# Opening of a hybrid layer: modulation weights of channel blocks 2 to 7 loaded and multiplied for two blocks at a time

## The chip, the cores and the metric

The kernel runs on one core of one Trainium2 chip. The metric is the device time of one execution in microseconds (us), as the median of several runs. A core has five engines that work at the same time and wait for each other through semaphores: TensorE (PE: matmuls into the PSUM memory; PEld in a profile is its loading of the stationary operand), VectorE (DVE), ScalarE (ACT), GpSimd (POOL) and SyncE (SP, which here only issues transfers). Each takes its instructions in the order in which they stand in its queue.

## The reference

One transformer layer on 512 tokens of 1024 channels, in float32: a gated FFN, a mixer of two attention-like branches, and a second gated FFN, each with its own norm and its own shift, scale and gate, that come from a condition vector c. The opening of the kernel computes the first lines of it:

```
mod = jax.nn.silu(c) @ w_ada + b_ada
sh1, sc1, g1, sh2, sc2, g2, sh3, sc3, g3 = [m[:, None, :] for m in jnp.split(mod, N_MOD, axis=-1)]
u = rms_norm(x, ffn1_norm_g) * (1 + sc1) + sh1
x = x + 0.5 * g1 * swiglu(u, ffn1_w_in, ffn1_w_out)
```

`w_ada` is 1024 x 9216. For the first norm the kernel needs only its first 2048 columns, those of sh1 and sc1: 8.4 MB.

## The kernel before

The 1024 channels are eight blocks k = 0 to 7 of 128, the 512 tokens four blocks of 128. The opening (`start`) runs through the channel blocks: it makes the normed, scaled and shifted input u of block k with channels on the partitions, and multiplies it by the rows k of the first three column blocks of both halves of `ffn1_w_in`, summing over k in six PSUM banks. All data are float32, and a matmul of float32 accuracy is made of three in a faster format, from high and low parts: `uh` and `ul` of u, `wh` and `wl` of the weights.

For one block k the steps are these, with the lines of the kernel before:

- SP loads `ar` (L710), the 1024 x 128 columns of `w_ada` for the shift and the same for the scale, as 128 partitions x 8 rows x 2 x 128 numbers, so in pieces of 512 bytes; and `raw` (L715), two pieces of 128 x 384 of the FFN weights.
- The product c times `ar` is a sum over 1024 rows. Its eight parts of 128 rows are multiplied by a number per partition and added up on DVE (L791 the first, L789 the others, one call for shift and scale together, 128 x 256), in a chain in which each call reads what the last one wrote; for some blocks ACT does the first part (L787). The sum over the 128 partitions is a matmul of the result by a column of ones, one each for shift and scale (`total`, L798). In blocks 1 and 2 some of the eight parts are summed by such matmuls on PE straight from `ar` (L780) and DVE has the others.
- ACT turns the two columns into shift and gain (`mods`, L802 and L803, 128 x 1 each).
- PE transposes the normed x of block k into a PSUM bank (`turn`, L748). ACT reads it twice, with the gain and the shift: into `uh` (L808, rounded) and `uf` (L809, full). DVE subtracts them: `ul` (L811).
- ACT rounds the FFN weights into `wh` (L815), DVE subtracts: `wl` (L819).
- PE does 18 matmuls of 128 x 512 (`mms`, L829): six with `uh` and `wh`, six with `uh` and `wl`, six with `ul` and `wh`.

The order of each engine's queue is written out by hand: each call is tied to follow the one before it on its engine (`queued`), so the text of `start` is the order. In the steady part (k from 3) PE's queue has the first six matmuls of block k-1, the transposes of block k, six more matmuls, `total(k)`, and the last six matmuls of block k-1, which run while ACT makes shift, gain and `uh` of block k. There is one free PSUM bank for the transposes. The four totals' columns of an even and an odd block lie side by side in one other bank (`cb`).

After the opening `cols_rest` transposes a few constants (L188), and the column blocks of the FFN follow, with matmuls at L115 to L117.

Of the kernel before, what the change touches and what calls it, by code (L numbers as in the profile page):

```python
# [20 lines left out]
P = 128  # L21
# [3 lines left out]
NK = 8  # L25
# [23 lines left out]
class Layer:  # L49
# [639 lines left out]
    def start(self, st, tp):  # L689
# [14 lines left out]
        ars, raws, accs, wsp, ms, bt = {}, {}, {}, {}, {}, {}  # L704
        def ada_load(k):
            r = ars[k] = st.tile([P, NK, 2, P], F32, name=self.nm("ar"), tag="ar", bufs=8)
            step = NK if k else 4
            for v in range(2):
                for i0 in range(0, NK, step):
                    spq(lambda: nc.sync.dma_start(r[:, i0:i0 + step, v, :], w_ada[i0 * P:(i0 + step) * P, v * D + k * P:v * D + (k + 1) * P]  # L710
                                                  .rearrange("(i p) n -> p i n", p=P)))
# [8 lines left out]
        ada_load(2)  # L720
# [56 lines left out]
        wide = lambda ap: ap.to_broadcast([P, P])  # L777
        def ada_pe(k, ks, v, first, last):
            for i in ks:
                pe(lambda: PE.matmul(cb[:, col(k, v):col(k, v) + P], ars[k][:, i, v, :], wide(self.ccol[:, i:i + 1]),  # L780
                                     start=first and i == ks[0], stop=last and i == ks[-1]))
        def product(k, i, eng):
            if not i:
                accs[k] = st.tile([P, 2, P], F32, name=self.nm("ac"), tag="ac", bufs=3)
            r, cc = ars[k][:, i], self.ccol[:, i:i + 1]
            if eng is AC:
                act(lambda: AC.activation(accs[k], r, AF.Copy, scale=cc))  # L787
            elif i:
                dve(lambda: V.scalar_tensor_tensor(accs[k], r, cc, accs[k], op0=MUL, op1=ADD))  # L789
            else:  # L790
                dve(lambda: V.tensor_scalar(accs[k], r, cc, None, op0=MUL))  # L791
# [3 lines left out]
        def total(k, more=()):  # L795
            for v in range(2):
                ada_pe(k, more, v, True, False)
                pe(lambda: PE.matmul(cb[:, col(k, v):col(k, v) + P], accs[k][:, v, :], wide(self.one), start=not more, stop=True))  # L798
# [6 lines left out]
        def uh(k):  # L805
            m = ms[k]
            uf[k] = self.tmp(tp, "uf")
            act(lambda: AC.activation(self.uh[k], bt[k], AF.Identity, scale=m[:, 1:2], bias=m[:, 0:1]))  # L808
            act(lambda: AC.activation(uf[k], bt[k], AF.Identity, scale=m[:, 1:2], bias=m[:, 0:1]))  # L809
# [52 lines left out]
        wl(1)  # L862
        wh(2)
        ada_dve(2, range(0, 2))
        ul(1)
        ada_dve(2, range(2, 6))
# [3 lines left out]
        mms(1, 6, 12)  # L870
        total(2, range(6, 8))
        wl(2)
        mods(2)
        uh(2)
        wh(3)
        ada_dve(3, range(0, 3))
        ul(2)
        wl(3)
        ada_dve(3, range(3, 8))
        mms(1, 12, 18)  # L880
        for k in range(3, NK):
            more, early = k < NK - 1, k > 3
# [3 lines left out]
            total(k)  # L886
            if more:
                product(k + 1, 0, AC)
                if early:
                    wh(k + 1)  # L890
                    wl(k + 1)
                ada_dve(k + 1, range(1, 4))
            mods(k)
            uh(k)
            ul(k)
            if more:
                if not early:
                    wh(k + 1)
                    wl(k + 1)
                ada_dve(k + 1, range(4, 8))  # L900
# [602 lines left out]
```

## Time and profile before

| | us |
|---|---|
| median of 3 runs | 1333.47 |
| lowest and highest | 1333.05, 1334.53 |
| the profiled execution | 1333.42 |
| its span, first to last instruction | 1331.6 |
| first matmul at L829 (block 0) | 16.87 |
| first matmul at L829 of block 2 | 30.26 |
| of block 4 | 43.73 |
| of block 6 | 54.66 |
| L188, behind the last matmul of the opening | 65.30 |

In a timeline each row has the start in us from the span's start, the length in us, the engine, the line, the operation, the tile it writes and those it reads, the shapes and how many instructions were put together; in brackets how long the engine stood idle before, and what ended that. A line "A <- B" of the waits says that A waited for B. Rows of groups have the count, the summed busy time, the mean length in ns, and the idle time before. PE's matmuls overlap: each shows about 0.39 us, while they start 0.23 us apart.

### The profile page before, as it was taken

The numbers are of one execution on the slowest core, as the hardware profiler recorded it, in microseconds if no ns is written. First come the engines' busy times: TensorE is split into PE (matmuls) and PEld (weight loads), VectorE is DVE, ScalarE is ACT, GpSimd is POOL, SyncE is SP. The second block draws the span as 40 slices with busy tenths as digits, with TensorE's granted clock in tenths as the row PEclk, the third lists the DMA queues.
The fourth block names the chain that finished last, engine by engine and source line by source line (L and its number), as shares of the span: only waits on it lengthen the run. The fifth ranks groups of instructions, "written<-read, shape, count | busy, mean of one in ns | idle before, by whom it ended". The sixth has DMA issues, their size and how long they took to land.

```text
span 1331.6 us, 17899 instructions
## 1 busy us (share of the span) xinstructions
PE 1312.8 (99%) x6468; PEld 1102.8 (83%) x6468; DVE 945.8 (71%) x1775; ACT 631.3 (47%) x1080; POOL 85.9 (6%) x140
## 2 busy tenths in 40 slices
PE   7999999999999999999999999999999999999998
PEld 6688888888888888988888878888888888888887
DVE  6777677688678867887685976777676565655655
ACT  5533433336557735566575686432354333433442
POOL 2000000001020000000000000002120000000000
PEclk9999999999999999999999999999999999999999
DMA  9776576777662434443343442787537555444474
GB/s 297 226 269 220 168 236 205 255 234 239 215 161 81 135 111 124 134 116 123 80 143 88 112 124 77 227 256 236 160 101 267 185 175 163 145 151 150 153 253 147
DMA packets 228621, 231.11 MB, mean 174 GB/s; under 512 B 12274, under 2 KB 183954, under 8 KB 228532
## 3 DMA queue, kind: packets, MB, share of 16 engines
q1 hardware_dynamic: 217428, 186.34, 46.4%
q0 software_dynamic: 11040, 43.61, 8.8%
q8 instruction: 51, 0.84, 0.2%
q14 instruction: 38, 0.31, 0.1%
q10 hardware_dynamic: 64, 0.02, 0.0%
HBM read 199.97 MB, written 29.95 MB: 173 GB/s over the span
## 4 chain that ended last, share of the span: by engine, by line
PE 91%; DVE 3%; ACT 2%; DMA 2%; issue 1%; SPq 0%; POOL 0%; ACTq 0%; DVEq 0%; POOLq 0%
PE g L117 21%; PE g L116 21%; PE g L115 21%; PE t L472 2%; PE t L474 2%; PE t L473 2%; PE t L1232 2%; PE t L446 1%; PE t L447 1%; PE t L445 1%; PE t L1202 1%; PE t L115 1%; PE t L117 1%; PE t L116 1%; PE g L829 1%
## 5 line engine op out<-in xcount | busy, mean ns | idle before, releaser
L96 ACT ACTIVATE wh<-raw 128x1024 fp32r<-128x1024 f32 x218 | 226.5, 1043 | 387.6 <-PE g L116 97.4
L116 PE MATMUL g<-ul,wh 128*128 128x512 f32 (+2 forms) x984 | 369.9, 376 | 1.1 <-DVE ul L255 0.8
L115 PE MATMUL g<-uh,wh 128*128 128x512 f32 (+2 forms) x984 | 370.1, 377 | 0.1
L117 PE MATMUL g<-uh,wl 128*128 128x512 f32 (+2 forms) x984 | 369.4, 376 | 0.2 <-DVE wl L98 0.2
L98 DVE TENSOR_TENSOR wl<-raw,wh 128x1024 fp32r<-128x1024 f32 x218 | 263.4, 1211 | 141.5 <-ACT wh L96 130.1
L116 PEld LDWEIGHTS g<-ul,wh 128*128 128x128 f32 (+1 forms) x984 | 185.0, 188 | 34.7 <-DVE ul L255 1.0
L117 PEld LDWEIGHTS g<-uh,wl 128*128 128x128 f32 (+1 forms) x984 | 184.9, 188 | 34.0 <-DVE wl L98 0.4
L115 PEld LDWEIGHTS g<-uh,wh 128*128 128x128 f32 (+1 forms) x984 | 184.7, 188 | 34.2 <-ACT sl L368 0.5
L115 PE MATMUL g<-wh,uh 128*128 128x512 f32 (+1 forms) x320 | 111.9, 350 | 0.0
L116 PE MATMUL g<-wl,uh 128*128 128x512 f32 (+1 forms) x320 | 111.0, 347 | 0.0
L117 PE MATMUL g<-wh,ul 128*128 128x512 f32 (+1 forms) x320 | 111.0, 347 | 0.0
L296 DVE SCALAR_TENSOR_TENSOR acc<-raw,ccol,acc 128x1024 f32<-128x1024 f32 (+1 forms) x63 | 66.0, 1065 | 43.0 <-DMA raw<-in_w_ada_dram 42.7
L117 PEld LDWEIGHTS g<-wh,ul 128*128 128x128 f32 x320 | 60.5, 189 | 7.8
L115 PEld LDWEIGHTS g<-wh,uh 128*128 128x128 f32 x320 | 60.5, 189 | 7.7 <-DVE tk L1085 0.5
L116 PEld LDWEIGHTS g<-wl,uh 128*128 128x128 f32 x320 | 60.5, 189 | 7.3
L369 DVE TENSOR_TENSOR hp<-g,sl 128x512 f32<-128x512 f32 x43 | 29.5, 689 | 51.6 <-PE g L117 50.8
L116 PE MATMUL g<-yl,wh 128*128 128x512 f32 x128 | 49.8, 389 | 0.0
L115 PE MATMUL g<-yl,wh 128*128 128x512 f32 x128 | 49.8, 389 | 0.0
L117 PE MATMUL g<-yl,wl 128*128 128x512 f32 x128 | 49.8, 389 | 0.0
L422 ACT ACTIVATE wh<-rw 128x1024 fp32r<-128x1024 f32 x22 | 23.3, 1058 | 49.0 <-issue 31.5
L1184 ACT ACTIVATE S<-S,mn 128x128 f32<-128x128 f32 (+1 forms) x64 | 35.5, 556 | 16.0 <-DVE mn L1176 8.9
L1446 POOL TENSOR_TENSOR sg<-sg,ta 128x512 f32<-128x512 f32 x8 | 13.6, 1694 | 452.4 <-DMA raw<-in_w_branch_b_dram 421.2
(339 smaller groups left out, 2252.1 us busy)
## 6 DMA issues: line engine op xcount, KB each, us to landing
raw<-in_ffn_w_in_dram SPq DMA_DIRECT2D x82, 512.0 KB, 4.7
raw<-in_w_ada_dram SPq DMA_DIRECT2D x56, 512.0 KB, 4.3
raw<-in_w_mix_dram SPq DMA_DIRECT2D x48, 512.0 KB, 3.9
rw<-in_ffn_w_out_dram POOLq DMA_DIRECT2D x20, 1024.0 KB, 6.8
S_d<-rw POOLq DMA_DIRECT2D x22, 768.0 KB, 4.0
raw<-S_d SPq DMA_DIRECT2D x30, 512.0 KB, 3.6
raw<-in_w_mix_dram SPq DMA_DIRECT2D x32, 256.0 KB, 3.9
ar<-in_w_ada_dram SPq DMA_DIRECT2D x14, 512.0 KB, 7.6
```

The source lines that it names most:

```text
L96: self.last_hi = nc.scalar.activation(hi, src, AF.Copy)
L98: self.last_lo = self.last_wl = (eng or nc.vector).tensor_tensor(lo, src, hi, op=SUB)
L115: mm(ps, lh, rh, start=start, stop=False)
L116: mm(ps, lh, rl, start=False, stop=False)
L117: self.last_mm = mm(ps, ll, rh, start=False, stop=stop)
L296: nc.vector.scalar_tensor_tensor(a, r[:, cut(i)], self.ccol[:, k:k + 1], a, op0=MUL, op1=ADD)
L369: nc.vector.tensor_tensor(h, ps_b[:, c0:c1], s[:, :c1 - c0], op=MUL)
L472: mm(ps[t], a[0], wh[:, k, :], start=first and c + k == 0, stop=False, skip_group_check=True)
L473: mm(ps[t], a[0], wl[:, k, :], start=False, stop=False, skip_group_check=True)
L474: mm(ps[t], a[1], wh[:, k, :], start=False, stop=end, skip_group_check=True)
L1184: nc.scalar.activation(S[:, ws], S[:, ws], AF.Exp, scale=-1.0, bias=m, accum_out=sm[:, qb:qb + 1])
L1232: nc.tensor.matmul(po[:, q0:], vt[pr][:, kb, i % 2, :], Px[:, o:o + T - q0], start=n == 1, stop=n == 8)
```

## The change

Blocks 2 and 3, 4 and 5, and 6 and 7 become pairs. The `ar` of a pair is one tile of 128 x 8 x 2 x 256, loaded by two transfers of 1 MB (one each for shift and scale), whose pieces are 1024 bytes long, in place of four transfers of 512 KB. It stands on SP's queue ahead of the FFN weights of both blocks. A product covers both blocks, 128 x 512 in place of 128 x 256, so there are eight per pair, not sixteen; ACT still does the first of pairs 4/5 and 6/7. The totals of both blocks follow each other on PE, and so do both `mods` on ACT. In the first pair DVE does six of the eight products (before, six for block 2 and all eight for block 3) and PE two for both blocks. The order of all four queues is rewritten to fit.

The core of the diff:

```diff
-        def ada_load(k):
-            r = ars[k] = st.tile([P, NK, 2, P], F32, name=self.nm("ar"), tag="ar", bufs=8)
+        def ada_load(*ks):
+            k, n = ks[0], len(ks) * P
+            r = st.tile([P, NK, 2, n], F32, name=self.nm("ar"), tag=f"ar{n}", bufs=2 if n == P else 3)
+            for i, kk in enumerate(ks):
+                ars[kk], accs[kk] = r[:, :, :, i * P:(i + 1) * P], (ks, i)
+            wide[k] = r
...
         def product(k, i, eng):
-            if not i:
-                accs[k] = st.tile([P, 2, P], F32, name=self.nm("ac"), tag="ac", bufs=3)
-            r, cc = ars[k][:, i], self.ccol[:, i:i + 1]
+            n = wide[k].shape[3]
+            if k not in acs:
+                acs[k] = st.tile([P, 2, n], F32, name=self.nm("ac"), tag=f"ac{n}", bufs=1 if n == P else 2)
+            r, cc = wide[k][:, i], self.ccol[:, i:i + 1]
...
-        def uh(k):
+        def uh(k, mid=lambda: None):
             m = ms[k]
             uf[k] = self.tmp(tp, "uf")
             act(lambda: AC.activation(self.uh[k], bt[k], AF.Identity, scale=m[:, 1:2], bias=m[:, 0:1]))
+            mid()
             act(lambda: AC.activation(uf[k], bt[k], AF.Identity, scale=m[:, 1:2], bias=m[:, 0:1]))
...
-        for k in range(3, NK):
-            ada_load(k)
-            if k < 6:
-                load(k)
-        load(6)
-        load(7)
+        load(3)
+        for k in (4, 6):
+            ada_load(k, k + 1)
+            load(k)
+            load(k + 1)
...
         wl(1)
+        ul(1)
+        ada_dve(2, range(0, 6))
         wh(2)
-        ada_dve(2, range(0, 2))
-        ul(1)
-        ada_dve(2, range(2, 6))
+        wh(3)
 
         mms(1, 0, 6)
         turn(2, range(NT))
-        mms(1, 6, 12)
-        total(2, range(6, 8))
+        mms(1, 6, 18)
+        total(2, (6, 7))
+        total(3, (6, 7))
+        mods(2)
+        mods(3)
         wl(2)
-        mods(2)
+        wl(3)
         uh(2)
-        wh(3)
-        ada_dve(3, range(0, 3))
         ul(2)
-        wl(3)
-        ada_dve(3, range(3, 8))
-        mms(1, 12, 18)
         for k in range(3, NK):
-            more, early = k < NK - 1, k > 3
             mms(k - 1, 0, 6)
             turn(k, range(NT))
             mms(k - 1, 6, 12)
-            total(k)
-            if more:
-                product(k + 1, 0, AC)
-                if early:
-                    wh(k + 1)
-                    wl(k + 1)
-                ada_dve(k + 1, range(1, 4))
-            mods(k)
-            uh(k)
-            ul(k)
-            if more:
-                if not early:
-                    wh(k + 1)
-                    wl(k + 1)
-                ada_dve(k + 1, range(4, 8))
+            if k % 2 == 0:
+                total(k)
+                total(k + 1)
+                mods(k)
+                mods(k + 1)
+            uh(k, lambda: product(k + 1, 0, AC) if k % 2 and k < NK - 1 else None)
+            if k % 2 and k < NK - 1:
+                wh(k + 1)
+                wh(k + 2)
+                ada_dve(k + 1, range(1, 3))
+                ul(k)
+                ada_dve(k + 1, range(3, 8))
+                wl(k + 1)
+                wl(k + 2)
+            else:
+                ul(k)
             mms(k - 1, 12, 18)
```

What the change moves shows best in the instruction lists of each engine's queue. The names carry running numbers. PE around the first totals of block 2, before: `uh_155`, `ul_163` and `wh_382` belong to block 1, `uh_156` to block 2, and `t_176` is the bank of the totals.

```order
L829 MATMUL t_175<-uh_155,wl_383 128x512
L780 MATMUL t_176<-ccol,ar_191 128x128 x2
L798 MATMUL t_176<-one,ac_416 128x128
L780 MATMUL t_176<-ccol,ar_191 128x128 x2
L798 MATMUL t_176<-one,ac_416 128x128
L829 MATMUL g_170<-ul_163,wh_382 128x512
L829 MATMUL g_171<-ul_163,wh_382 128x512
L829 MATMUL g_172<-ul_163,wh_382 128x512
L829 MATMUL g_173<-ul_163,wh_382 128x512
L829 MATMUL t_174<-ul_163,wh_382 128x512
L829 MATMUL t_175<-ul_163,wh_382 128x512
L829 MATMUL g_170<-uh_156,wh_413 128x512
```

And now:

```order
L835 MATMUL t_175<-ul_163,wh_373 128x512
L784 MATMUL t_176<-ccol,ar_191 128x128 x2
L803 MATMUL t_176<-one,ac_405 128x128
L784 MATMUL t_176<-ccol,ar_191 128x128 x2
L803 MATMUL t_176<-one,ac_405 128x128
L784 MATMUL t_176<-ccol,ar_191 128x128 x2
L803 MATMUL t_176<-one,ac_405 128x128
L784 MATMUL t_176<-ccol,ar_191 128x128 x2
L803 MATMUL t_176<-one,ac_405 128x128
L835 MATMUL g_170<-uh_156,wh_412 128x512
```

The last six matmuls of block 1 moved ahead of the totals, and the totals of block 3 stand behind those of block 2, right before the matmuls of block 2.

DVE from `ul` of block 3 to the products of block 5, before (`ac_493` is block 4's sum, `ac_538` block 5's):

```order
L811 TENSOR_TENSOR ul_165<-uf_501,uh_157 128x512
L819 TENSOR_TENSOR wl_506<-raw_344,wh_505 128x768
L789 SCALAR_TENSOR_TENSOR ac_493<-ar_341,ccol,ac_493 128x256 x4
L819 TENSOR_TENSOR wl_541<-raw_350,wh_540 128x768
L789 SCALAR_TENSOR_TENSOR ac_538<-ar_347,ccol,ac_538 128x256 x3
L811 TENSOR_TENSOR ul_166<-uf_550,uh_158 128x512
L789 SCALAR_TENSOR_TENSOR ac_538<-ar_347,ccol,ac_538 128x256 x4
```

And now, from `ul` of block 2, with `ac_484` the sum of the pair 4/5:

```order
L817 TENSOR_TENSOR ul_164<-uf_461,uh_156 128x512
L794 SCALAR_TENSOR_TENSOR ac_484<-ar_338,ccol,ac_484 128x512 x2
L817 TENSOR_TENSOR ul_165<-uf_482,uh_157 128x512
L794 SCALAR_TENSOR_TENSOR ac_484<-ar_338,ccol,ac_484 128x512 x5
L825 TENSOR_TENSOR wl_488<-raw_341,wh_487 128x768
L825 TENSOR_TENSOR wl_491<-raw_344,wh_490 128x768
L817 TENSOR_TENSOR ul_166<-uf_536,uh_158 128x512
```

All seven products of a pair on DVE now stand between `ul` of one even block and `wl` of the next, with `ul` of the odd block among them.

ACT now, from the pair 2/3 to the pair 4/5:

```order
L807 ACTIVATE m_453<-t_176,colC 128x1
L808 ACTIVATE m_453<-t_176,colC 128x1
L807 ACTIVATE m_456<-t_176,colC 128x1
L808 ACTIVATE m_456<-t_176,colC 128x1
L813 ACTIVATE uh_156<-t_424,m_453 128x512
L815 ACTIVATE uf_461<-t_424,m_453 128x512
L813 ACTIVATE uh_157<-t_471,m_456 128x512
L792 ACTIVATE ac_484<-ar_338,ccol 128x512
L815 ACTIVATE uf_482<-t_471,m_456 128x512
L821 ACTIVATE wh_487<-raw_341 128x768
L821 ACTIVATE wh_490<-raw_344 128x768
L807 ACTIVATE m_530<-t_176,colC 128x1
```

Four small steps now stand ahead of the first `uh` of a pair, and the first product of the next pair (`ac_484`) stands between `uh` and `uf` of the odd block.

More of the change, by code (lines that the diff above doesn't have):

```diff
@@ L703, in start @@
         sh = [P, 2, NJ0 * P]
-        ars, raws, accs, wsp, ms, bt = {}, {}, {}, {}, {}, {}
-        def ada_load(k):
-            r = ars[k] = st.tile([P, NK, 2, P], F32, name=self.nm("ar"), tag="ar", bufs=8)
+        ars, raws, accs, wsp, ms, bt, wide, acs = {}, {}, {}, {}, {}, {}, {}, {}
+        def ada_load(*ks):
[4 more added lines that the diff above has]
+            wide[k] = r
             step = NK if k else 4
@@ L709, in ada_load @@
                 for i0 in range(0, NK, step):
-                    spq(lambda: nc.sync.dma_start(r[:, i0:i0 + step, v, :], w_ada[i0 * P:(i0 + step) * P, v * D + k * P:v * D + (k + 1) * P]
+                    spq(lambda: nc.sync.dma_start(r[:, i0:i0 + step, v, :], w_ada[i0 * P:(i0 + step) * P, v * D + k * P:v * D + k * P + n]
                                                   .rearrange("(i p) n -> p i n", p=P)))
@@ L719, in start @@
         load(1)
-        ada_load(2)
+        ada_load(2, 3)
         load(2)
@@ L797, in total @@
                 ada_pe(k, more, v, True, False)
-                pe(lambda: PE.matmul(cb[:, col(k, v):col(k, v) + P], accs[k][:, v, :], wide(self.one), start=not more, stop=True))
+                pe(lambda: PE.matmul(cb[:, col(k, v):col(k, v) + P], acs[accs[k][0][0]][:, v, accs[k][1] * P:(accs[k][1] + 1) * P], bcast(self.one), start=not more, stop=True))
         def mods(k):
```

10 lines of the change are left out of this document (5 added, 5 removed).

## The prediction

> **What bounds the kernel now.** First the span, then who waits in the opening (16 to 65 us of the span, where the change lies), then one round of it in order of time.
>
> ```profile
> span 1331.6 us, 17899 instructions
> ```
>
> ```profile
> ACT m L802 <- PE t L798: 18.1, 7, 3.5
> DVE ul L811 <- ACT uf L809: 8.5, 8, 2.8
> PEld g L829 <- ACT uh L808: 4.5, 8, 1.4
> PEld t L798 <- DVE ac L789: 4.0, 5, 1.8
> ...
> DVE ac L791 <- DMA ar<-in_w_ada_dram: 1.8, 2, 1.6
> ...
> ACT ac L787 <- DMA ar<-in_w_ada_dram: 0.8, 1, 0.8
> ```
>
> The columns are total us, times, longest. The large entries are engines waiting for engines. The modulation weights (ar) delay someone by only 2.6 us. So transfers do not pace the opening; a ring of engines does. One turn of it, block 5 to block 6, from the timeline (start, length):
>
> ```profile
> 47.08 0.71 PE L798 MATMUL t<-one,ac 128*128 128x128 f32 x4
> ...
> 49.84 0.69 DVE L811 TENSOR_TENSOR ul<-uf,uh 128x512 fp32r<-128x512 f32 x1 [0.51 <-ACT uf L809]
> 50.45 2.04 DVE L789 SCALAR_TENSOR_TENSOR ac<-ar,ccol,ac 128x256 f32<-128x256 f32 x4
> 52.55 0.52 PEld L798 LDWEIGHTS t<-one,ac 128*128 128x128 f32 x4 [0.29 <-DVE ac L789]
> ```
>
> A turn lasts 52.55 - 47.08 = 5.47 us: total on PE, m and uh on ACT, ul and four products on DVE, next total. PE has nearly as much work, so its weight load waits only 0.29. Behind the opening PE is full, as this window shows (length of the window, then busy time of PE, PEld, DVE, ACT and POOL, granted clock, share of the DMA engines, GB/s), so whatever the opening loses or gains passes to the end.
>
> ```profile
> 90.00:100.00 10.00, 10.00 (x46) 8.29 (x45) 5.21 (x6) 2.61 (x3) 0.00 (x0) 1.00 0.68 250
> ```
>
> **The first pair: weights, products, totals.** The change first differs at block 2. Rows of the timeline of before:
>
> ```profile
> 19.45 0.85 ACT L815 ACTIVATE wh<-raw 128x768 fp32r<-128x768 f32 x1 [0.74 <-DMA raw<-in_ffn_w_in_dram]
> 22.85 0.35 DVE L791 TENSOR_SCALAR ac<-ar,ccol 128x256 f32<-128x256 f32 x1 [1.56 <-DMA ar<-in_w_ada_dram]
> 24.66 0.69 DVE L811 TENSOR_TENSOR ul<-uf,uh 128x512 fp32r<-128x512 f32 x1 [0.94 <-ACT uf L809]
> 27.13 0.64 PEld L780 LDWEIGHTS t<-ccol,ar 128*128 128x128 f32 x4
> 28.58 0.76 PEld L829 LDWEIGHTS g<-ul,wh 128*128 128x128 f32 x4
> 28.89 0.26 ACT L802 ACTIVATE m<-t,colC 128x1 f32<-128x1 f32 x1 [3.33 <-PE t L798]
> 29.05 0.34 ACT L803 ACTIVATE m<-t,colC 128x1 f32<-128x1 f32 x1
> 29.42 0.78 ACT L808 ACTIVATE uh<-t,m 128x512 fp32r<-128x512 f32 x1
> 30.26 1.20 PE L829 MATMUL g<-uh,wh 128*128 128x512 f32 x4
> ```
>
> Both 19.45 and 22.85 are landings, since the engine waited for the DMA. Nothing lies between them on SP's queue but block 2's weights, 2 x 524,288 bytes: 1.049 MB in 3.40 us, 308 GB/s at pieces of 512 bytes. Now 2.097 MB must land in that place, in pieces of 1024 bytes. At 308 GB/s that takes 6.81 us. For wider pieces the stretches of before say (columns as in the window above):
>
> ```profile
> 38.00:42.00 4.00, 3.13 (x17) 2.30 (x17) 3.85 (x7) 1.73 (x3) 0.00 (x0) 1.00 1.20 290
> 70.00:71.00 1.00, 1.00 (x6) 0.84 (x5) 1.00 (x3) 0.00 (x0) 0.00 (x0) 1.00 1.15 346
> 484.00:485.00 1.00, 1.00 (x6) 0.81 (x5) 0.96 (x3) 0.41 (x3) 0.00 (x0) 1.00 1.06 371
> ```
>
> The first is the opening's weights at 512 bytes, the second FFN weights at 512 bytes, the third the mixer's weights at 1024 bytes (blocks 128 x 2 x 256). I take 340, the middle between 308 and 371: 6.17 us, landing at 25.62. At 371 it would be 25.10, but DVE is in ul(1) until 24.66 + 0.69 = 25.35, so 25.35 is the floor; at 308 it is 26.26.
>
> The Trainium skill, page "DMA: Bandwidth & Descriptors", section "Specifications", puts the smallest transfer for line rate at 512 B; by that rule doubling the piece gains nothing, and the sum below would end at +3.0 us instead of +2.4. The stretches quoted side against it only partly: 371 is above 290, but 346 shows 512-byte pieces nearly as fast elsewhere.
>
> Next the products. The trace has no dependent 128x512 product with ar; by form it has these:
>
> ```profile
> L789 DVE SCALAR_TENSOR_TENSOR ac<-ar,ccol,ac 128x256 f32<-128x256 f32 x43 | 20.7, 484 | 1.2
> L960 DVE SCALAR_TENSOR_TENSOR cy<-cz,colA,cy 128x512 f32<-128x512 f32 x24 | 17.1, 741 | 0.0
> L296 DVE SCALAR_TENSOR_TENSOR acc<-raw,ccol,acc 128x512 f32<-128x512 f32 x28 | 21.2, 796 | 7.0 <-DMA raw<-in_w_ada_dram 6.9
> L536 DVE SCALAR_TENSOR_TENSOR rs<-rs,gb 128x512 f32<-128x512 f32 x12 | 8.1, 687 | 3.5 <-DMA gb<-mod_d 3.4
> L298 DVE TENSOR_SCALAR acc<-raw,ccol 128x512 f32<-128x512 f32 x4 | 1.8, 480 | 0.0
> L743 ACT ACTIVATE xn<-x,rq 128x512 f32<-128x512 f32 x4 | 2.6, 710 | 0.0
> ```
>
> Four dependent products of 256 last 2.04 us, so each start is (2.04 - 0.484)/3 = 0.519 after the last: its length plus 0.035. For 512 I take 741 ns (scalar from a column, all in SBUF, as here) plus 0.035, 0.776 us. Bounds are 687 and 796 plus the same. Doubling the width costs 0.776 against 2 x 0.519 = 1.04, so DVE does less work in all; what counts is that one chain is longer.
>
> First pair: 0.48 + 0.035 + 5 x 0.776 = 4.40 us after 25.62 gives 30.02, and PE sees it about 0.05 later, 30.07. By then PE has finished all 18 matmuls of block 1 (12 by 27.13, as before, and the last six by about 28.5) and stands, since the six that used to hide the m and uh steps now lie ahead of the totals. Of the 12 totals matmuls, two need only ar and run early. Six took 28.58 - 27.13 = 1.45 us, so the other ten take 2.42. m follows PE's end by 28.89 - 28.58 = 0.31. I let m(2) wait for both totals, as they write one bank. Four m steps at 29.05 - 28.89 = 0.16 make 0.64, and uh to the first matmul takes 30.26 - 29.42 = 0.84. Block 2's matmuls start at 30.07 + 2.42 + 0.31 + 0.64 + 0.84 = 34.28, 4.02 us later than at 30.26.
>
> **The turns of the pairs.** Some of that returns, as total(3) is already done. Rows:
>
> ```profile
> 35.13 0.71 PE L798 MATMUL t<-one,ac 128*128 128x128 f32 x4 [1.39 <-DVE ac L789]
> 35.60 1.17 PE L829 MATMUL g<-ul,wh 128*128 128x512 f32 x4
> 35.88 0.26 ACT L802 ACTIVATE m<-t,colC 128x1 f32<-128x1 f32 x1 [2.91 <-PE t L798]
> ...
> 43.73 1.19 PE L829 MATMUL g<-uh,wh 128*128 128x512 f32 x4
> 45.22 0.60 PE L748 MATMUL t<-ident,xn 128*128 128x128 f32 x4
> 45.57 1.17 PE L829 MATMUL g<-uh,wl 128*128 128x512 f32 x4
> ...
> 54.66 1.19 PE L829 MATMUL g<-uh,wh 128*128 128x512 f32 x4
> ...
> 62.34 0.40 PE L829 MATMUL g<-ul,wh 128*128 128x512 f32 x1
> ...
> 64.39 0.39 PE L829 MATMUL t<-ul,wh 128*128 128x512 f32 x1
> ...
> 65.30 0.26 PE L188 MATMUL t<-ident,rowsA 112*128 112x112 f32 x1
> ```
>
> From the first matmul of an even block to the next pair's total: the odd block's transposes end 45.22 + 0.60 - 43.73 = 2.09 later, uh follows at 2.13, the ACT product 0.68 after it (an estimate: a little under uh's own 0.78, since ACT overlaps its steps), DVE starts 0.71 + 0.05 after that, at 3.57. Then two products (1.55), ul (0.61, from 49.84 to 50.45), five products (3.88) and 0.05: 9.66. From total to the next even block: m after two totals 35.88 - 35.13 = 0.75, two further totals 35.60 - 35.13 = 0.47, four m steps 0.64, uh to matmul 0.84: 2.70. A pair's turn is 12.36 us. Before, two blocks took 54.66 - 43.73 = 10.93.
>
> PE's own work in that turn reaches the total after 7.8 us: 6 matmuls with transposes 45.57 - 43.73 = 1.84, twice, and 18 matmuls at 0.23, since nine start within 64.39 - 62.34 = 2.05 without a wait (0.228). So PE stands 1.8 us per pair, waiting for products. It also lacks cover for the second pair of m steps.
>
> Blocks 4 and 6 start at 34.28 + 12.36 = 46.64 and 59.00. What follows is two blocks without totals: 1.84 + 30 x 0.23 = 8.74, as uh and ul of block 7 now come early enough. The end of the opening is 67.74. Before it is 65.30: **+2.4 us**.
>
> What is free: wl, wh and the other loads. Weights of pair 4/5 follow two blocks of FFN weights (0.79 MB, at most 2.6 us) and their own 6.8, so land by about 35.6 even at 308 GB/s; ACT asks at 34.28 + 2.81 = 37.1. If that cover of 1.5 us went, uf(3), both wh and with uf(3) the transposes behind on PE would be late by the excess. On SP's queue, load(5) waits for wl(2), which DVE reaches at 30.02, and holds back the last pair's weights; these have until 46.64 + 2.81 = 49.4, some 18 us, so the 7 us of transfer fit. POOL's w_out loads wait for the last m on ACT; it now stands two blocks ahead of the end of the opening instead of one, so they get more time. The buffers take 3 x 16 KB plus 2 x 8 KB against 8 x 8 KB for each partition, the same 64.
>
> **Sum.** 1333.42 us for the profiled execution (span 1331.6 and 1.8 around it) plus 2.4 is 1335.8; with the median shown 0.05 above the profiled execution, **1335.9**. This is slower by 0.18%, so just within the 0.2%, 2.7 us, which is about what a measurement tells from no change.
>
> **Rivals.**
>
> *Cheaper pieces.* Landing at the floor 25.35 saves 0.27, and 687 ns products save 19 x 0.054 = 1.03. Then +1.1, 1334.6. For it: the 371 stretch. Against: 687 is a product by an immediate number.
>
> *Wide pieces no faster, products dear.* At 308 GB/s the landing adds 0.64, products at 796 ns add 19 x 0.055 = 1.05: +3.0 with the first alone, +4.1 with both, 1336.5 to 1337.6, slower. For it: 308 measured on these same weights, and 796 with the same weight tensor in another shape. Against: the 796 group's lengths mix with waits for its loads.
>
> *TensorE's clock falls.* PE would stand about 1.0 us before the totals at 30.07 and 1.8 before block 2, with little between. If the clock halved there, some seven matmuls would cost 0.23 more each: +1.6, +4.0 in all, 1337.5. It decides at an idle longer than any of before: there PEld's longest wait for products, 1.8 us, left the clock at 1.00 in the window from 38 to 42. The Trainium skill, "TensorE: Matmul & The Clock Gate", Part 1, puts the drop after an idle window of about 3.4 us; by that rule it stays away, and the granted clock of before agrees.
>
> *PE, not the chain, sets the pace.* Should a wide product cost what a narrow one does, 0.519, the chain to the total shrinks by 7 x 0.257 to 7.86, which is PE's 7.8. Then 2 x 1.8 and 5 x 0.257 = 1.3 are saved: -2.5, 1331.0, and with a little more it is faster. Against: every 512 row above costs 0.2 more.
>
> *The change acts on nothing that counts.* Waits even out, 1333.5 to 1334. The order of work speaks against: the totals do move behind the last six matmuls.
>
> **Chances.** Forecast 0.62 (three quarters of it inside 0.2%), cheaper pieces or nothing that counts 0.10, dear 0.17, clock 0.06, PE's pace 0.05 (0.03 of it faster). Within 0.2%: 0.46 + 0.10 + 0.02 = 0.58; slower 0.16 + 0.17 + 0.06 = 0.39; faster 0.03. The range, 1333.7 to 1337.6, takes in the cheap and the dear bounds; below lies only PE's pace.
>
> **What would show it.** Right: ar of 2 and 3 landing near 25.6; 128x512 products about 0.74 us long; the first totals near 30, block 2 near 34.3; PE waiting for products about 1.8 us at the totals of 4 and 6, and these two 12.4 apart; no wait for ul at block 7. Wrong: DVE products done before PE asks, a granted clock under 1.00, ACT waiting for ar at product(4), or PE gaps after the opening that take up the loss.

## The result and the profile after

The changed kernel takes 1336.42 us in the median of 21 runs (1335.38 to 1337.45), the kernel before 1333.63 us in 21 runs beside it (1332.63 to 1334.90). The ratio is 1.0021, with a 95% interval of 1.0015 to 1.0027: slower by 2.8 us. The forecast was 1335.9 us, within 1333.7 to 1337.6.

The profiled execution of the changed kernel took 1335.7 us, with a span of 1333.9 us.

The waits of the changed kernel in the opening (16 to 68 us of its span; total us, times, longest):

```profile
ACT m L807 <- PE t L803: 16.8, 4, 5.1
DVE ul L817 <- ACT uf L815: 12.9, 6, 3.4
PEld t L803 <- DVE ac L794: 5.7, 3, 2.0
...
DVE ac L794 <- ACT ac L792: 4.5, 2, 2.3
...
DVE ac L796 <- DMA ar<-in_w_ada_dram: 1.2, 2, 0.9
```

L803 is now the total (L798 before), L794 the product on DVE (L789), L792 the product on ACT, L807 the first step of `mods` (L802), L835 the 18 matmuls (L829). The ring of engines is the same, with fewer and longer waits: ACT waits for totals four times instead of seven, and up to 5.1 us. The entry `DVE ac <- ACT ac` is new: DVE stands 2.3 us per pair until ACT has done the pair's first product. The wait of PE's weight load (PEld) for products grew from 4.0 to 5.7 us. DVE's wait for weights, 1.2 us, is no longer than before.

The first pair in the timeline of the changed kernel:

```profile
19.02 0.85 ACT L821 ACTIVATE wh<-raw 128x768 fp32r<-128x768 f32 x1 [0.71 <-DMA raw<-in_ffn_w_in_dram]
25.88 0.49 DVE L796 TENSOR_SCALAR ac<-ar,ccol 128x512 f32<-128x512 f32 x1 [0.94 <-DMA ar<-in_w_ada_dram]
26.41 3.90 DVE L794 SCALAR_TENSOR_TENSOR ac<-ar,ccol,ac 128x512 f32<-128x512 f32 x5
30.36 0.49 PE L803 MATMUL t<-one,ac 128*128 128x128 f32 x2 [1.46 <-DVE ac L794]
32.90 0.26 ACT L807 ACTIVATE m<-t,colC 128x1 f32<-128x1 f32 x1 [4.21 <-PE t L803]
34.51 1.19 PE L835 MATMUL g<-uh,wh 128*128 128x512 f32 x4 [1.66 <-ACT uh L813]
```

Weights land at 25.88, products are done at 30.31, m(2) starts only behind the totals of both blocks, and block 2's matmuls begin at 34.51, where they began at 30.26 before. The next two turns, to L188 behind the last matmul of the opening:

```profile
37.38 0.71 ACT L792 ACTIVATE ac<-ar,ccol 128x512 f32<-128x512 f32 x1
38.12 1.54 DVE L794 SCALAR_TENSOR_TENSOR ac<-ar,ccol,ac 128x512 f32<-128x512 f32 x2 [2.27 <-ACT ac L792]
...
40.18 3.89 DVE L794 SCALAR_TENSOR_TENSOR ac<-ar,ccol,ac 128x512 f32<-128x512 f32 x5
44.12 0.97 PEld L803 LDWEIGHTS t<-one,ac 128*128 128x128 f32 x8 [2.01 <-DVE ac L794]
46.94 1.19 PE L835 MATMUL g<-uh,wh 128*128 128x512 f32 x4 [0.27 <-ACT uh L813]
...
59.38 1.20 PE L835 MATMUL g<-uh,wh 128*128 128x512 f32 x4 [0.26 <-ACT uh L813]
...
68.18 0.26 PE L188 MATMUL t<-ident,rowsA 112*128 112x112 f32 x1
```

Blocks 2, 4 and 6 start 12.43 and 12.44 us apart, and in each turn PE's weight load stands 2.0 us for the pair's products. PE itself stands 1.58 us there, as its last matmuls still run when the load begins to wait. L188 comes at 68.18 instead of 65.30, +2.88. The span grew by 2.3 only; the other 0.6 us goes somewhere in the 1266 us behind the opening, and no single place was found for it. It is less than the 2.07 us by which the runs of the kernel differ.

| | before | after | predicted |
|---|---|---|---|
| products of the first pair start | 22.85 (block 2 alone) | 25.88 | 25.62 |
| block 2 starts | 30.26 | 34.51 | 34.28 |
| block 4 starts | 43.73 | 46.94 | 46.64 |
| block 6 starts | 54.66 | 59.38 | 59.00 |
| L188 | 65.30 | 68.18 | 67.74 |

### The profile page after: what moved, and what is told of

The parts are those of the page before. It is cut to its first block, busy times and chain, and to the rows that moved or that the text cites. A ratio compares the mean times of both kernels' runs of the same rounds, so it can differ in the third digit from the quotient of the medians.

```text
span 1333.9 us, 17884 instructions
## 1 busy us (share of the span) xinstructions
PE 1312.3 (98%) x6476; PEld 1105.3 (83%) x6476; DVE 939.4 (70%) x1753; ACT 630.3 (47%) x1078; POOL 85.6 (6%) x140
## 4 chain that ended last, share of the span: by engine, by line
PE 93%; DVE 2%; ACT 2%; SPq 1%; DMA 1%; issue 1%; POOL 0%; ACTq 0%; DVEq 0%; POOLq 0%
PE g L117 22%; PE g L116 22%; PE g L115 22%; PE t L472 2%; PE t L474 2%; PE t L473 2%; PE t L1235 2%; PE t L446 1%; PE t L445 1%; PE t L447 1%; PE t L1205 1%; PE t L115 1%; PE t L117 1%; PE t L116 1%; DVE ac L794 1%; PE t L1176 1%
```

## The experiments

All kernels here were timed against the kernel before (medians of 1333.36, 1333.63 and 1333.22 us in the three sets). "Against its own set" below means that each kernel's median is first set against the median of before in the same set; the changed kernel is 2.8 us slower by that measure. Where block 0's first matmul starts at different times in two profiles (16.3 to 17.4 us, which no edit below touches), the text says so or uses differences within one profile. Such a difference need not carry through to the end: where products wait for weights, the landing sets their time.

**The products of a pair started two blocks earlier.** The theory is that the loss of each turn is the product chain, which may start only behind `uh` of the odd block. The edit lets ACT's product and three of DVE's seven run behind the even block's `ul`:

```diff
-            uh(k, lambda: product(k + 1, 0, AC) if k % 2 and k < NK - 1 else None)
+            uh(k)
             if k % 2 and k < NK - 1:
                 wh(k + 1)
                 wh(k + 2)
-                ada_dve(k + 1, range(1, 3))
                 ul(k)
-                ada_dve(k + 1, range(3, 8))
+                ada_dve(k + 1, range(4, 8))
...
             else:
                 ul(k)
+                if k < NK - 2:
+                    ahead(k + 2)
```

Here `ahead(k)` is `product(k, 0, AC)` and `ada_dve(k, range(1, 4))`; `ahead(4)` also stands behind `ul(2)`.

> The changed kernel with one move: the first product of a pair on ACT and three of the seven on DVE are issued right behind uf and ul of the even block before, not behind uh of the odd block. Theory (the product chain sets each pair's turn): in the changed kernel DVE stands 2.3 us per pair until ACT's product (rows at 38.12 and 50.55), so the totals of 4 and 6 come about 2.0 us earlier, PE's wait for them falls from 2.0 to about 0, and each turn goes from 12.4 to about 10.4 us: about -4.1 us, 1332.3 us, ratio to the kernel before 0.9990. Rival (PE's own work or the loads set the pace): the turn stays near 12.4 and the time at 1336.4, ratio 1.0021.

Measured: 1332.74 us, ratio 0.9997 (0.9988 to 1.0006), 3.4 us under the changed kernel against its own set. Block starts in the timeline of this kernel:

```profile
34.95 1.20 PE L835 MATMUL g<-uh,wh 128*128 128x512 f32 x4 [1.66 <-ACT uh L813]
...
45.53 1.19 PE L835 MATMUL g<-uh,wh 128*128 128x512 f32 x4 [0.27 <-ACT uh L813]
...
56.12 1.20 PE L835 MATMUL g<-uh,wh 128*128 128x512 f32 x4 [0.27 <-ACT uh L813]
```

The turns are 10.58 and 10.59 us in place of 12.43 and 12.44, 3.7 us in all, though block 2 starts no earlier. In its waits (16 to 68 us) PE's weight load waits for products once, ahead of the first totals, and not for those of 4 and 6:

```profile
PEld t L803 <- DVE ac L794: 1.8, 1, 1.8
```

The gain came out of the order of the product chain alone; the weights, tiles and instructions are those of the changed kernel. The rival (that PE's own work or the loads set the turn) falls.

**The same pair tile, loaded in narrow pieces.** Four transfers of 512 KB in pieces of 512 bytes per pair, in place of two of 1 MB in pieces of 1024 bytes:

```diff
-            for v in range(2):
-                for i0 in range(0, NK, step):
...
+            for c0 in range(0, n, P):
+                for v in range(2):
+                    for i0 in range(0, NK, step):
+                        spq(lambda: nc.sync.dma_start(r[:, i0:i0 + step, v, c0:c0 + P],
+                                                      w_ada[i0 * P:(i0 + step) * P, v * D + k * P + c0:v * D + k * P + c0 + P]
...
```

> The changed kernel, but each pair's weights come in four transfers of 512 KB with pieces of 512 bytes, in place of two of 1 MB with pieces of 1024 bytes. Theory (the wide pieces move at about 354 GB/s against 308): the weights of pair 2/3 land 0.5 to 0.9 us later, and as nothing covers that, the time rises by as much: about 1337.1 us, ratio to the kernel before 1.0026; the later pairs have cover and change nothing. Rival (pieces of 512 bytes are already at line rate): landing and time stay, 1336.4, 1.0021.

Measured: 1337.45 us, ratio 1.0037 (1.0024 to 1.0051). In the timeline, and then in the window from 16 to 30 us (columns as in the prediction; the last is GB/s):

```profile
19.52 0.85 ACT L823 ACTIVATE wh<-raw 128x768 fp32r<-128x768 f32 x1 [0.64 <-DMA raw<-in_ffn_w_in_dram]
...
27.39 0.49 DVE L798 TENSOR_SCALAR ac<-ar,ccol 128x512 f32<-128x512 f32 x1 [1.85 <-DMA ar<-in_w_ada_dram]
```

```profile
16.00:30.00 14.00, 12.44 (x68) 10.23 (x68) 7.97 (x14) 7.09 (x12) 0.00 (x0) 1.00 1.09 303
```

The same window of the changed kernel, in the first row, and of the next kernel but one (by halves of the rows), in the second. That one has four transfers of 512 KB for the first pair too, but pieces of 1024 bytes:

```profile
16.00:30.00 14.00, 12.43 (x68) 10.23 (x68) 8.68 (x14) 6.79 (x11) 0.00 (x0) 1.00 1.10 359
...
16.00:30.00 14.00, 13.22 (x75) 11.04 (x76) 9.55 (x16) 6.66 (x11) 0.00 (x0) 1.00 1.10 359
```

The landing is 1.51 us later. The landing of the FFN weights before it is 0.50 later in this profile (19.52 against 19.02), which leaves 1.01 for the pieces. With PE equally busy, 1024-byte pieces move 359 GB/s and 512-byte pieces 303; the number of transfers makes no difference to the rate. The rate is the safer of the two figures. In other profiles that load the pair by the same two transfers and in which DVE waits for them, the time between these two landings is 6.29 us (`pairs_filled`) to 7.34 us (`early_product`), 6.86 in the changed kernel and 7.87 here. The medians alone would not show it: against its own set this kernel is 1.3 us above the changed one, and the intervals overlap. The Trainium skill, page "DMA: Bandwidth & Descriptors", section "Specifications", has line rate from 512 B on; the two rows disagree by 18%, and the measurement decides here.

**The last six matmuls of block 1 put back behind the totals.** The prediction said that they no longer hide the m and uh steps.

```diff
-        mms(1, 6, 18)
+        mms(1, 6, 12)
         total(2, (6, 7))
         total(3, (6, 7))
+        mms(1, 12, 18)
```

> The changed kernel, but the last six matmuls of block 1 go back behind the totals of blocks 2 and 3 on PE. Theory (block 2 starts when totals, four m steps and uh are through, whatever PE does meanwhile): PE's idle moves from behind the totals (1.66 us) to ahead of them, block 2 starts within 0.1 us of 34.5, and the time stays at 1336.4, ratio 1.0021. Rival (as the prediction put it, the six matmuls no longer hide the m and uh steps): the 1.4 us that they take come back, 1335.0, 1.0010.

Measured: 1336.46 us, ratio 1.0025 (1.0016 to 1.0034): no difference. The totals and block 2 in its timeline:

```profile
30.38 0.49 PE L803 MATMUL t<-one,ac 128*128 128x128 f32 x2 [1.86 <-DVE ac L794]
...
34.53 1.19 PE L835 MATMUL g<-uh,wh 128*128 128x512 f32 x4 [0.26 <-ACT uh L813]
```

From the first total to block 2 it takes 4.15 us, as in the changed kernel (30.36 to 34.51). (Block 0 starts 0.98 later in this profile, at 17.44; the products of the first pair then follow `ul(1)` at 25.90 without a wait for weights.) PE's stand of 1.66 before block 2 became one of 0.26, and block 2 starts no earlier: the chain through ACT sets it. So moving those six matmuls cost nothing, and the 1.4 us of the rival do not come back.

**The first pair's weights by halves of their rows.** Rows 0 to 511 of shift and scale land first, so that products 0 to 3 can run while the rest is on its way (block 0 keeps its order):

```diff
-            step = NK if k else 4
-            for v in range(2):
-                for i0 in range(0, NK, step):
...
+            step = 4 if k in (0, 2) else NK
+            for i0, v in [(i0, v) for i0 in range(0, NK, step) for v in range(2)] if k else [(i0, v) for v in range(2) for i0 in (0, 4)]:
...
```

> The changed kernel, but the weights of pair 2/3 are loaded as four transfers of 512 KB, rows 0 to 511 of shift and scale first, then rows 512 to 1023, so that DVE can begin when half has landed; the pieces stay 1024 bytes. Theory (the landing of the whole pair at 25.9 us delays the first totals): products start when DVE is through with ul(1), near 24.9 in place of 25.9, and block 2 and the end come about 0.9 us earlier, 1335.5 us, ratio 1.0014. Rival (the landing does not count): no difference, 1.0021.

Measured: 1335.16 us, ratio 1.0014 (1.0005 to 1.0023), 1.0 us under the changed kernel against its own set; the two intervals overlap, so the timeline has to carry the argument. Its products and block 2:

```profile
24.71 0.48 DVE L795 TENSOR_SCALAR ac<-ar,ccol 128x512 f32<-128x512 f32 x1
...
33.34 0.96 PE L834 MATMUL g<-uh,wh 128*128 128x512 f32 x3 [1.66 <-ACT uh L812]
```

The product waits for no DMA any more (no bracket) and follows `ul(1)`. It starts 1.17 us earlier than in the changed kernel, and block 2 by the same 1.17 (0.13 of it since block 0 starts at 16.33 here). So the part of the landing that lies behind `ul(1)`, 0.94 us in the profile of the changed kernel, is on the path, and block 2 gets all of it back. How large this part is changes from profile to profile: with the same transfers it is 1.06 us in `early_product`, 0.44 in `pairs_filled` and none in the kernel with the last six behind.

**The loads alone.** The kernel before, with pair tiles loaded as in the changed kernel, but every product, total and `mods` block by block:

```diff
-        ada_load(2)
+        ada_load(2, 3)
         load(2)
...
-        for k in range(3, NK):
-            ada_load(k)
...
+        load(3)
+        for k in (4, 6):
+            ada_load(k, k + 1)
+            load(k)
+            load(k + 1)
```

> The kernel before, with only the loading of the change: weights of blocks 2 and 3, 4 and 5, 6 and 7 by two transfers of 1 MB each in the change's order on SP's queue; products, totals and all other queues as before, 128x256 products reading half of the wide tile. Theory (block 2 now waits for the bytes of block 3 too): the weights land near 25.9 us instead of 22.9, block 2's products end near 29.5 instead of 27.3, and every later turn moves by that: about +2.2 us, 1335.6 us, ratio to the kernel before 1.0017. Rival (the loads have cover, only the order of the engines' work costs): no difference, 1.0000.

Measured: 1335.73 us, ratio 1.0015 (1.0007 to 1.0024). DVE stands long for the weights, where its products are as narrow as before:

```profile
26.42 0.35 DVE L794 TENSOR_SCALAR ac<-ar,ccol 128x256 f32<-128x256 f32 x1 [5.33 <-DMA ar<-in_w_ada_dram]
...
29.90 0.49 PE L801 MATMUL t<-one,ac 128*128 128x128 f32 x2 [2.05 <-DVE ac L792]
...
33.09 1.84 PE L832 MATMUL g<-uh,wh 128*128 128x512 f32 x4
```

Waiting for two blocks' weights where one block's would do costs 2.1 us by itself, although the transfers are the faster ones. The 2.1 us hold two other things. In the order of before, `ul(1)` stands behind two of the products, so it is done only after the landing and adds 0.6 us to the chain (27.20 to 27.81). And the four matmuls at 33.09 take 1.84 us instead of 1.20: the granted clock falls here too, behind PE's wait of 2.05 us (windows as above, the clock behind the five engines):

```profile
30.00:32.00 2.00, 2.00 (x12) 1.80 (x13) 1.93 (x4) 0.87 (x3) 0.00 (x0) 0.83 1.09 349
32.00:34.00 2.00, 2.00 (x7) 1.52 (x6) 0.87 (x3) 1.82 (x3) 0.00 (x0) 0.50 1.09 386
34.00:36.00 2.00, 2.00 (x11) 1.66 (x10) 1.93 (x4) 0.51 (x1) 0.00 (x0) 0.82 1.07 372
```

In this profile the slow matmuls delay nothing further on, as the weight load of block 3's totals behind them waits 0.55 us for products. How much of the 2.1 us between the medians is the clock is not shown: in four of the eleven executions the mean clock is 1.000, and their median is 1335.0 us, 1.4 above before.

**The late pairs alone.** Blocks 2 and 3 as in the kernel before, one at a time; blocks 4/5 and 6/7 as pairs:

```diff
-        ada_load(2, 3)
+        ada_load(2)
         load(2)
...
+        ada_load(3)
         load(3)
         for k in (4, 6):
...
+            if k == 3:
+                total(3)
+                mods(3)
```

> The kernel before for blocks 0 to 3, with loads and products in single blocks, and the change for pairs 4/5 and 6/7 only (wide loads, wide products, totals one behind the other, ACT's first product behind uh of the odd block). Theory: block 2 starts as before (30.3 us), block 3 near 37.3, then seven wide products follow uh(3), so the totals of 4 and 5 come near 43.9 instead of 41.6; the turn from 4 to 6 takes 12.4 instead of 10.9 and the stretch behind 6 takes 8.8 instead of 10.6: about +2.5 us, 1335.9, ratio 1.0019. Rival (only the first pair costs, the later pairs are neutral): 1333.4, 1.0000.

Measured: 1337.98 us, ratio 1.0030 (1.0018 to 1.0042), 2 us more than expected. The totals of 4 and 5 came as forecast, but what followed did not. Timeline, then windows of this kernel (the column behind the five engines is the granted clock):

```profile
43.44 1.16 PE L803 MATMUL t<-one,ac 128*128 128x128 f32 x8 [3.11 <-DVE ac L794]
44.35 1.82 PE L835 MATMUL g<-ul,wh 128*128 128x512 f32 x4
...
57.22 1.16 PE L803 MATMUL t<-one,ac 128*128 128x128 f32 x8 [1.89 <-DVE ac L794]
58.13 1.93 PE L835 MATMUL g<-ul,wh 128*128 128x512 f32 x4
```

```profile
44.00:46.00 2.00, 2.00 (x11) 1.64 (x10) 1.12 (x2) 1.37 (x5) 0.00 (x0) 0.66 0.31 84
46.00:48.00 2.00, 2.00 (x6) 1.61 (x5) 0.69 (x1) 0.87 (x2) 0.00 (x0) 0.50 0.84 261
48.00:50.00 2.00, 2.00 (x12) 1.60 (x12) 0.00 (x0) 0.21 (x1) 0.00 (x0) 0.99 0.41 122
```

Four matmuls take 1.82 and 1.93 us instead of 1.17, and the clock is at 0.66 and 0.50. That is the rival of the prediction about TensorE's clock, in a kernel where PE itself waits 3.11 us instead of 1.58. Three more kernels were run to find out whether the wait was the cause.

**The same, with PE kept busy.** Extra matmuls of 128x512 (`fill`, with their count) ahead of a pair's totals, into the totals' bank, whose results the totals overwrite:

```diff
             if k % 2 == 0:
+                fill(k - 1, 12 if k == 4 else 7)
                 total(k)
                 total(k + 1)
```

> The kernel in which only the pairs 4/5 and 6/7 are pairs, with extra matmuls put on PE where it waits for the pair's products: 12 of 128x512 ahead of totals 4/5 (at 0.228 us each 2.7 of the 3.11 us that it waits) and 7 ahead of totals 6/7 (1.6 of 1.89). They write the columns that the totals then overwrite. Theory (PE standing idle brings the granted clock down): the clock is 1.00 in every window of the opening, groups of four matmuls take 1.17 to 1.20 us again, block 4 starts 44.35 + 0.2 + 1.1 + 1.2 = about 46 at latest (46.8 with the drop), blocks 4 and 6 stand 12.4 apart, and the median is 2 us under that of the late pairs without filling: 1336.0, ratio 1.0018. Rival (the clock falls there for another reason, such as the sudden work of all engines at once): the clock again falls under 0.8 behind totals 4/5, the turn is 13.9, and the median stays at 1338, ratio 1.0030 or more.

Measured: 1335.99 us, ratio 1.0020 (1.0012 to 1.0029). Timeline and window:

```profile
44.55 1.16 PE L803 MATMUL t<-one,ac 128*128 128x128 f32 x8 [0.36 <-DVE ac L794]
45.46 1.17 PE L835 MATMUL g<-ul,wh 128*128 128x512 f32 x4
```

```profile
44.00:46.00 2.00, 1.64 (x11) 1.38 (x11) 2.00 (x3) 0.26 (x2) 0.00 (x0) 1.00 0.02 6
```

Nineteen more matmuls made this kernel 2.0 us faster (1.6 us against its own set). The clock stays at 1.00, and from block 0's first matmul to L188 it takes 68.88 - 17.24 = 51.64 us instead of 69.85 - 16.46 = 53.39. Block 4 came at 47.36, later than the 46 expected: the sum given there (44.35 + 0.2 + 1.1 + 1.2) is 46.85, and this profile's opening starts 0.8 later. Blocks 4 and 6 stand 12.75 apart, not the 12.4 expected; why stays open. The executions agree with the profile: the mean clock is 0.997 in four of the six of the late pairs alone, and 0.999 or 1.000 in all eleven here. That the waits of PE brought the clock down is shown by this; the rival falls.

**The changed kernel, with PE kept busy.** Seven such matmuls ahead of totals 4/5 and 6/7 of the changed kernel (the same line with `fill(k - 1, 7)`).

> The changed kernel with seven extra matmuls of 128x512 (1.6 us) on PE ahead of totals 4/5 and again ahead of totals 6/7, where it waits 2.0 us each time. Theory (the clock stays up in the changed kernel, and its loss is the chain alone): nothing changes, turns of 12.4, granted clock 1.00, median 1336.4, ratio 1.0021 within 0.0006. Rival (in a part of the executions the clock falls after these waits, and the median holds some of that): the median comes out 0.7 us or more lower, 1335.7, ratio 1.0016 or less.

Measured: 1336.89 us, ratio 1.0027 (1.0016 to 1.0037). Nothing is gained: the ratio is not below the changed kernel's 1.0021, and the two intervals overlap. The executions say the same: in eleven of the changed kernel's 21 the mean clock is 1.000, and their median is 1336.52 us, no lower than that of all. So the changed kernel's loss has no clock in it.

**The changed kernel with a longer chain.** `ul(3)` is done three times over, so that the last five products of pair 4/5 come 1.2 us later:

```diff
-                ul(k)
+                for _ in range(3 if k == 3 else 1):
+                    ul(k)
                 ada_dve(k + 1, range(3, 8))
```

> The changed kernel with the subtraction that makes ul of block 3 done three times over (same result, two more instructions of 0.61 us on DVE ahead of the last five products of pair 4/5), so that PE waits 2.0 + 1.2 = 3.2 us ahead of totals 4/5. If a wait of this length brings the clock down, as it seemed with the late pairs alone: granted clock under 0.8 in the windows behind totals 4/5, block 4 at 46.94 + 1.2 + 1 to 2, and the median 2.2 to 3.2 above the changed kernel, 1338.6 to 1339.6 (ratio 1.0037 to 1.0045). If not: block 4 at 48.15, the clock 1.00, and the median 1.2 above, 1337.6 (ratio 1.0030).

Measured: 1339.02 us, ratio 1.0042 (1.0029 to 1.0054). Timeline and windows:

```profile
45.92 1.16 PE L803 MATMUL t<-one,ac 128*128 128x128 f32 x8 [3.03 <-DVE ac L794]
46.84 1.73 PE L835 MATMUL g<-ul,wh 128*128 128x512 f32 x4
```

```profile
46.00:48.00 2.00, 2.00 (x12) 1.77 (x13) 1.61 (x2) 0.88 (x5) 0.00 (x0) 0.80 0.11 18
48.00:50.00 2.00, 2.00 (x6) 1.59 (x5) 0.61 (x1) 1.36 (x3) 0.00 (x0) 0.50 0.85 259
50.00:52.00 2.00, 2.00 (x11) 1.61 (x10) 0.08 (x1) 0.06 (x1) 0.00 (x0) 0.84 0.63 187
```

1.2 us more on DVE cost 2.6 us between the medians (3.0 against its own set), and the clock falls 1.3 us behind the end of the wait of 3.03 us.

**Both gains together.** The earlier products and the weights by halves, each as above.

> Both moves that gained, together: the changed kernel with the first products of the next pair behind uf and ul of the even block, and the weights of pair 2/3 in halves of the rows. Theory: the two gains lie one behind the other on the path (first totals 1.2 us earlier, then two turns near 10.6) and add up: about 1331.5 us, ratio to the kernel before 0.9985. Rival (once the turns are set by PE, an earlier first pair is given back by PE's work or by the landing of pair 4/5): 1332.7, 0.9997 as with the first move alone.

Measured: 1331.70 us, ratio 0.9986 (0.9977 to 0.9995): faster than the kernel before by 1.9 us and than the changed kernel by 4.7. Blocks 4 and 6 and L188 in its timeline:

```profile
44.18 1.19 PE L834 MATMUL g<-uh,wh 128*128 128x512 f32 x4 [0.27 <-ACT uh L812]
...
54.77 1.20 PE L834 MATMUL g<-uh,wh 128*128 128x512 f32 x4 [0.27 <-ACT uh L812]
...
63.54 0.26 PE L188 MATMUL t<-ident,rowsA 112*128 112x112 f32 x1
```

Turns are 10.6 us, and L188 comes 1.76 us earlier than before (block 0 starts 0.36 earlier in this profile).

## Why the prediction was right, step by step

**What bounds the opening: right.** The ring of engines, not the transfers. Starting the products of a turn earlier took 3.7 us out of the opening with the same transfers.

**The landing: the mechanism right, the size off.** The prediction took 340 GB/s and 6.17 us between the FFN weights' landing and that of the pair. The rows say 25.88 - 19.02 = 6.86 us, or 306 GB/s, at the bound it had named (308). It ended only 0.26 us later than forecast on the span's scale, because this profile's opening began 0.41 us earlier; that part of the agreement is luck. The reason is not that wide pieces are no faster: the narrow ones took 1.01 us longer. The prediction used 308 GB/s, measured between two landings of narrow pieces, and raised it for the width; but the 2.1 MB in narrow pieces would have needed 27.39 - 19.52 = 7.87 us between the same two landings, 266 GB/s. The DMA engines were not slower than forecast: between 19.02 and 25.88 they moved 361 GB/s, 2.48 MB in all, of which the pair's weights are 2.10. In the stretch from which 308 was taken, they moved 315 GB/s, 1.07 MB, of which 1.05 are block 2's. What was off is that the prediction put all bytes moved between two landings down to what lands. Which transfers the other 0.38 MB belong to, and why the stretch takes 6.29 us in one profile and 7.34 in another, stays open.

**The products: right.** 0.776 us from start to start were forecast, from 741 ns and 0.035 of gap. The group by form has

```profile
L794 DVE SCALAR_TENSOR_TENSOR ac<-ar,ccol,ac 128x512 f32<-128x512 f32 x19 | 14.3, 751 | 5.1 <-ACT ac L792 4.5
```

751 ns, and five in 3.90 us are (3.90 - 0.751) / 4 = 0.787 from start to start. The price per product was nearly met by the row of 741 ns; the bounds were 687 and 796.

**Totals to block 2: the sum right, one sentence wrong.** Forecast were 4.21 us from totals to block 2 (two blocks' totals, four m steps, uh), and they took 4.15. The totals for both blocks do stand ahead of m(2). But the prediction also said that PE stands "since the six that used to hide the m and uh steps now lie ahead of the totals", as if that were part of the loss. With those six behind the totals, the time did not change. The chain through ACT was counted in full and the six matmuls were not, so the number stood in spite of the sentence.

**The turns: right.** 12.36 us were forecast and 12.43 and 12.44 measured; 1.8 us of waiting for products per pair were forecast, and the weight load waits 2.0, PE itself 1.58. The last stretch was to take 8.74 and took 68.18 - 59.38 = 8.80.

**The free parts: right.** Nobody waits for the weights of pairs 4/5 and 6/7: DVE's two waits for weights, 1.2 us in all, are those of block 1 and the first pair.

**The sum.** +2.4 us were forecast at L188. Measured are +2.88 on the span's scale: 0.26 from the landing, 0.15 from the two turns, 0.06 from the end and 0.03 from the products, less 0.06 from totals to block 2. The median moved by 2.8, against 2.4 in the forecast. Counted from block 0's first matmul, the profile shows more: (68.18 - 16.46) - (65.30 - 16.87) = 3.29 us. In two kernels whose edits changed nothing, the same difference is 2.34 us (the last six behind) and 2.82 us (the changed kernel with PE kept busy), so one profile gives the loss of the opening to about half a microsecond. The agreement of the sum is real in its terms and partly luck in its last tenths. The ratio lies at the edge of what the prediction called no change (0.2%): 0.18% was forecast, with a chance of 0.58 for staying within 0.2%, and 0.21% was measured.

**How the parts combine.** Late pairs alone with the clock held up cost 2.8 us (1335.99 against 1333.22), loads alone 2.1, the whole change 2.8. They don't add up. The likely reason, which no run singles out, is that each delays the same ring, and that a pair that starts late finds total(3) done.

**The rivals.** *Wide pieces no faster, products dear* has its first half as a size (306 GB/s) but not as a cause, and its second half not at all (751 ns, not 796). *Cheaper pieces*, *PE sets the pace* and *nothing that counts* fall with the turn of 12.43 us, the 751 ns and the landing. *TensorE's clock falls* didn't happen in the changed kernel: keeping PE busy gains nothing there, and behind its waits for the pairs' products the windows have the full clock. It happens in neighbours of this kernel whose wait at PE is 0.3 to 1.5 us longer (1.89, 2.05, 3.03 and 3.11 us against 1.58), though not in every such one. The windows of the changed kernel behind its totals 4/5 and 6/7:

```profile
44.00:46.00 2.00, 1.87 (x12) 1.74 (x13) 1.81 (x3) 0.68 (x4) 0.00 (x0) 1.00 0.03 5
...
58.00:60.00 2.00, 1.74 (x8) 1.09 (x7) 0.25 (x1) 2.00 (x6) 0.00 (x0) 1.00 0.69 197
```

## What to carry to other kernels

Merging two steps of a ring made fewer and cheaper instructions here but a longer chain, and the chain is what counted: before merging, ask when its first link may start, and move that start ahead by as much as the chain grows. Load a merged operand in the order in which it is used (here by halves of its rows), so that the first use doesn't wait for all of it. Where an edit makes the matmul engine wait for about 2 us or more, look at the granted clock in the windows behind the wait: slower matmuls may come on top of it.

## What the runs showed of the hardware

**A half clock after a wait.** Behind PE's waits of 3.11 and 3.03 us, and of 2.05 us in the kernel with the loads alone, the granted clock fell to a half. In windows of a quarter of a microsecond it is 0.50 or 1.00, with other values only where it changes. So the half-clock time in the windows from 44 to 50 us of the late pairs alone is 2 x 2.0 x (0.34 + 0.50 + 0.01) = 3.4 us, in those from 46 to 52 us of the longer chain 2 x 2.0 x (0.20 + 0.50 + 0.16) = 3.4 us, and in those from 30 to 36 us of the loads alone 2 x 2.0 x (0.17 + 0.50 + 0.18) = 3.4 us. The slow stretch does not begin in the wait but 1.0 to 1.4 us behind its end. An estimate from these lengths: PE loses half of 3.4, about 1.7 us, when it has work throughout, and less where a wait follows. The Trainium skill, page "TensorE: Matmul & The Clock Gate", Part 1, has windows of about 3.4 us that run freely: one idle window halves the clock, one busy one restores it. The length of the slow stretch agrees. The wait that starts it doesn't quite: 2.05 us sufficed, and in the late pairs alone even the second wait, of 1.89 us at PE, was followed by a slow stretch (the matmuls at 58.13 above). Waits at PE of 1.58 us in the changed kernel, 1.86 us in the kernel with the last six behind, of 1.56 us in the longer chain (first row) and even of 2.37 us with the narrow pieces (second row) were not:

```profile
59.38 1.16 PE L803 MATMUL t<-one,ac 128*128 128x128 f32 x8 [1.56 <-DVE ac L794]
...
31.86 0.49 PE L805 MATMUL t<-one,ac 128*128 128x128 f32 x2 [2.37 <-DVE ac L796]
```

So the length of the wait alone does not decide. Nor does the kernel alone: with the loads alone the mean clock of an execution is 1.000 in four of eleven and 0.998 in three. What else decides, and whether the first slow stretch prepares the second, stays open.

**Pieces of 1024 bytes move faster than pieces of 512 bytes** from the same weights into the same tile: 303 GB/s from 16 to 30 us with narrow pieces, against 357 to 360 in the eight profiles that load the first pair in pieces of 1024 bytes. Between the landings this made 1.01 us on 2.1 MB.
